# Two-layer hybrid encoder on one core: 512-column and 256-column matmuls of a weight piece sorted into runs

## The chip, the core and the metric

The kernel runs on 1 core of one Trainium2 chip. The metric is the device time of one execution in microseconds (us). Before the change the median of three runs is 747.52 us (747.17 to 747.56). Columns, partitions and shapes are written as the profile writes them: 128x512 is 128 partitions by 512 elements.

## What is computed

A hidden state of 256 tokens by 1024 features goes through two layers. The first has a mixer of two attention groups (windowed attention, and latent attention behind low-rank inputs), the second a mixer of three dilated attention windows. Each is followed by an MLP with a squared ReLU, and a last RMS norm ends it. All data are float32.

```python
def reference(x, ...):
    for layer in range(DEPTH):                       # DEPTH = 2
        xn = rms_norm(x, norm_mix[layer])
        if layer % 2 == 0:
            x = x + even_mixer(xn, ...)
        else:
            x = x + odd_mixer(xn, ...)
        x = x + sq_relu_mlp(rms_norm(x, norm_mlp[layer]), mlp_w1[layer], mlp_w2[layer])
    return rms_norm(x, norm_final)

def sq_relu_mlp(xn, w1, w2):                         # 1024 -> 4096 -> 1024
    return jnp.square(jax.nn.relu(xn @ w1)) @ w2

def odd_mixer(xn, w_in, w_o, cos_f, sin_f):          # queries, keys, values of 3 groups, 16 heads
    hcat = (xn @ w_in).reshape(b, s, DIL_GROUPS, 3, DIL_HEADS, HEAD_DIM)
    q = apply_rope(hcat[:, :, :, 0], cos_f, sin_f)
    k = apply_rope(hcat[:, :, :, 1], cos_f, sin_f)
    return dilated_attention(q, k, hcat[:, :, :, 2]) @ w_o
```

## The kernel before

**Split products.** Every float32 operand is split into a high part (rounded to the matmul type fp32r) and a low part (what is left), and a product is the sum of three: high by high, high by low and low by high. `split` makes the parts of a weight: a ScalarE copy (L201, "CAST whi<-raw") and then a VectorE subtraction (L202, "TENSOR_TENSOR wlo<-raw,whi"), in four parts of 512 columns for each weight piece of 128x2048. `weight()` hands out the next piece and lets the loads and splits run ahead of it; there are 4 buffers for raw pieces and 3 for each of whi and wlo. The loads are issued on SyncE's queue (SP).

**Two ways to issue the three products.** `mm3` (L205 to L207) issues three matmuls. Where the activations are the moving operand, two of the three can be one: `pair_tile` keeps the high and the low activations side by side, so that a single matmul of 512 columns gives whi by high in columns 0 to 255 of a PSUM bank and whi by low in columns 256 to 511, and a second matmul of 256 columns adds wlo by high to columns 0 to 255. This pair is used in two places:

- `up(j)` in `mlp` (L390 and L391), the MLP's first product: 16 weight pieces for each layer, and for each of them two banks (f = 0 and 1) with 8 pairs each (k = 0 to 7), 512 pairs in all. When a bank is done, ScalarE copies columns 256 to 511 out (L394, "side"), VectorE adds the two halves (L395, "u"), squares the positive part (L397) and splits it (L201 and L202, hh and hl).
- `gemm` in the `qk_steps` of `odd` (L905 and L906), the queries and keys of the second layer: 24 weight pieces, for each two banks with 8 pairs, 384 pairs in all. A bank's 8 pairs are cut into two steps of 4 (`half`), and other work is put between steps.

**Order.** Each engine executes its instructions in one fixed order. It comes from the order in which the code is written, changed by the scheduler of the framework, which moves instructions that could not start yet in its own model of time behind others that could. In the MLP it is `up(0)`, `up(1)`, `up(2)`, and then the second product of piece j (`down`, 24 matmuls of 512 columns through `mm3`) and `up(j + 3)` in turn. At the start of an MLP, `hand_over` adds the last products to the residual stream and prepares the activations in four blocks of two k (`join`: L301 on VectorE, then L241 on ScalarE for the high parts and L242 on VectorE for the low parts); `up(0)` therefore takes k in three ranges. In `odd`, `weave` puts the attention of one unit (scores L214 and L971, softmax, transposes L991, and `mix`, L1002 and L1007) between the steps that make the next unit's queries, keys and values.

**Other places that the change touches.** In `even`, `c_tail` normalises the low-rank inputs (L568, "cn") and returns a step that transposes them on TensorE (L576) and splits them (ch and cl). The list `main` holds the steps of this layer with a weight in time for each; the two transposing steps stand ahead of `main` and in its second place. `mix` in `odd` takes one PSUM bank for each half of the tokens. `finish` ends the kernel: the last 128 tokens are multiplied by the gain as they come (L504, "xg"), and when the reciprocal root of the norm is there (L232, on GpSimd), VectorE scales columns 0 to 511 (L506) for a store on SP's queue (L507), and ScalarE scales columns 512 to 1023 (L508) for a store on its own queue (L509).

Of the kernel before, what the change touches and what calls it, by code (L numbers as in the profile page):

```python
# [16 lines left out]
F32 = mybir.dt.float32  # L17
# [6 lines left out]
P = 128  # L24
# [44 lines left out]
def trunk(ctx, tc, a, out):  # L69
# [304 lines left out]
    def mlp(mp, xT, s, invert, tail, make_down, beside=lambda j: None):  # L374
# [4 lines left out]
        def up(j):  # L379
            w = weight()  # L380


            pu = [bank("w") for _ in range(2)]

            ranges = [range(4), range(4, 6), range(6, 8)] if j == 0 else [range(8)]
            for ks in ranges:
                for f in range(2):
                    for k in ks:
                        c = slice(k * 256 + f * P, k * 256 + f * P + P)
                        nc.tensor.matmul(two(pu[f]), w[0][:, c], xT[2][:, k], start=k == 0, stop=False)  # L390
                        nc.tensor.matmul(pu[f][:, 0:T], w[1][:, c], xT[0][:, k, :], start=False, stop=k == KT - 1)  # L391
# [48 lines left out]
    def finish(mp, xT, s):  # L440
# [49 lines left out]
        xg = [scratch([512], "xg") for _ in range(2)]  # L490
        residual(1, HALF[1], accs[3])
        for i, (c0, c1) in enumerate(((0, 512), (512, 768), (768, D))):
# [11 lines left out]
            nc.vector.tensor_tensor(xg[c0 // 512][:, c0 % 512:c0 % 512 + c1 - c0], v, g[:, c0:c1], op=ALU.mult)  # L504
        r = rsqrt(ss[:, 3:4], "x")
        nc.vector.tensor_scalar(xg[0], xg[0], r, None, ALU.mult)  # L506
        nc.sync.dma_start(out[P:T, HALF[0]], xg[0])  # L507
        nc.scalar.activation(xg[1], xg[1], AF.Copy, scale=r)  # L508
        nc.scalar.dma_start(out[P:T, HALF[1]], xg[1])  # L509


    def even(ep):
# [289 lines left out]
        turn_c[0]()  # L802
# [4 lines left out]
        main.insert(1, (0, turn_c[1]))  # L807
# [19 lines left out]
    def odd(op, xT, s):  # L827
# [64 lines left out]
        def qk_steps(d, js=QK_ORDER):  # L892
# [4 lines left out]
            def gemm(b, f, half):  # L897
# [5 lines left out]
                for k in range(4 * half, 4 * half + 4):  # L903
                    ws = slice((f * KT + k) * P, (f * KT + k + 1) * P)
                    nc.tensor.matmul(two(pq), wh[:, ws], xp[:, k], start=k == 0, stop=False)  # L905
                    nc.tensor.matmul(pq[:, 0:T], wl[:, ws], xh[:, k, :], start=False, stop=k == KT - 1)  # L906
# [51 lines left out]
        def attention(u, d):  # L958
# [36 lines left out]
            def mix(out_tag):  # L995
                pvo = [bank(out_tag) for _ in range(NT)]
                v0, v12 = values_of(u)
                for i in range(NT):
                    for kk in range(NT):
                        for j in range(2):  # L1000
                            cs = slice(64 * j, 64 * j + 64)
                            nc.tensor.matmul(pvo[i][cs, 0:P], v0[:, kk, cs], turned[i, j][:, kk, :], start=kk == 0, stop=False)  # L1002
                    for c in range(2):
                        qs = slice(64 * c, 64 * c + 64)
                        for j in range(2):
                            cs = slice(64 * j, 64 * j + 64)
                            nc.tensor.matmul(pvo[i][cs, qs], v12[:, 2 * i + c, cs], turned[i, j][:, 2, qs], start=False, stop=c == 1)  # L1007
                with tc.high_priority(NORM_PRIO):
                    for i in range(NT):
# [153 lines left out]
```

## Time and profile before

| what | value |
|---|---|
| median of three runs | 747.52 us |
| the profiled execution's own time | 746.66 us |
| its span, first to last instruction | 744.8 us |
| TensorE (PE) | 737.3 us busy, 99% of the span, 4539 matmuls |
| VectorE (DVE) | 539.9 us, 72% |
| ScalarE (ACT) | 473.6 us, 64% |
| GpSimd (POOL) | 8.3 us, 1% |
| granted TensorE clock, mean | 0.999 |
| HBM | 127.16 MB read, 172 GB/s over the span |

How to read what follows. A row of the timeline has the start of an instruction (or of several of one kind, merged, with their count), how long it took, and its line and operands. Matmuls are pipelined: one starts while the one before it is still in the array, so the busy time of a matmul (0.39 us for 512 columns) is longer than the distance to the next one's start. Since the profile models the ends of matmuls, all arithmetic on matmuls uses distances from start to start, called steps here. PEld is the engine row of the weight loads: every matmul has one of its own.

### The profile page before, as it was taken

Reading aid. Unit: us, or ns where it says so; the run is one execution under the profiler, and the core shown is the slowest. Engines: PE = TensorE matmul, PEld = TensorE weight load, DVE = VectorE, ACT = ScalarE, POOL = GpSimd, SP = SyncE. Lnnn points to the kernel's source line nnn. Section 1 sums busy time; section 2 is a strip of 40 time slices with the busy share of each in tenths; the row PEclk is TensorE's granted clock in tenths of the full one; section 3 lists DMA queues with packets and bytes.
Section 4 is the critical chain, followed back from the end, with each engine's and each line's share of the span. In section 5 each row is a group of like instructions: output and inputs, shape, how many; then the busy total and the mean of one; then the engine's idle time right before and its main releaser. Section 6 shows DMA issues by size and latency. Waiting matters only on the chain.

```text
span 744.8 us, 12006 instructions
## 1 busy us (share of the span) xinstructions
PE 737.3 (99%) x4539; PEld 634.8 (85%) x4539; DVE 539.9 (72%) x1109; ACT 473.6 (64%) x1027; POOL 8.3 (1%) x20
## 2 busy tenths in 40 slices
PE   9999999999999999999999999999999999999996
PEld 7998998888888887888888888888898888888885
DVE  6778858766666667689968886899558765665664
ACT  7788866554554556468877768687856544554541
POOL 0100000000000001000000000000000000000000
PEclk9999999999999999999999999999999999999999
DMA  9772334565555554645654555455545556555501
GB/s 292 309 272 97 118 113 166 175 222 178 187 201 178 191 196 152 234 159 172 213 209 144 191 175 180 136 194 169 194 148 181 194 191 205 184 177 191 193 13 56
DMA packets 24585, 133.17 MB, mean 179 GB/s; under 512 B 3664, under 2 KB 4688, under 8 KB 10192
## 3 DMA queue, kind: packets, MB, share of 16 engines
q1 hardware_dynamic: 24384, 132.15, 51.4%
q8 instruction: 35, 0.57, 0.3%
q10 hardware_dynamic: 144, 0.26, 0.1%
q14 instruction: 22, 0.18, 0.1%
HBM read 127.16 MB, written 1.05 MB: 172 GB/s over the span
## 4 chain that ended last, share of the span: by engine, by line
PE 97%; issue 1%; ACT 1%; DVE 0%; POOLq 0%; POOL 0%
PE w L390 16%; PE acc L205 13%; PE acc L207 13%; PE acc L206 13%; PE acc L905 12%; PE w L391 8%; PE acc L906 6%; PE acc L553 3%; PE w L214 1%; PE w L991 1%; PE w L205 1%; PE w L207 1%; PE w L763 1%; PE w L206 1%; PE w L971 1%
## 5 line engine op out<-in xcount | busy, mean ns | idle before, releaser
L202 DVE TENSOR_TENSOR wlo<-raw,whi 128x512 fp32r<-128x512 f32 (+2 forms) x471 | 304.6, 680 | 128.7 <-ACT whi L201 128.0
L201 ACT CAST whi<-raw 128x512 fp32r<-128x512 f32 (+2 forms) x471 | 262.4, 615 | 173.4 <-PE w L390 62.4
L390 PE MATMUL w<-pair,whi 128*128 128x512 f32 x512 | 182.2, 397 | 0.0
L391 PE MATMUL w<-pair,wlo 128*128 128x256 f32 x512 | 144.2, 282 | 0.0
L905 PE MATMUL acc<-pair,whi 128*128 128x512 f32 x384 | 139.2, 403 | 0.0
L390 PEld LDWEIGHTS w<-pair,whi 128*128 128x128 f32 x512 | 96.5, 189 | 23.1
L906 PE MATMUL acc<-pair,wlo 128*128 128x256 f32 x384 | 108.1, 282 | 0.0
L205 PE MATMUL acc<-whi,hh 128*128 128x512 f32 x250 | 98.2, 393 | 0.0
L207 PE MATMUL acc<-whi,hl 128*128 128x512 f32 x250 | 97.9, 391 | 0.0
L206 PE MATMUL acc<-wlo,hh 128*128 128x512 f32 x250 | 97.8, 391 | 0.0
L391 PEld LDWEIGHTS w<-pair,wlo 128*128 128x128 f32 x512 | 96.1, 188 | 0.9
L905 PEld LDWEIGHTS acc<-pair,whi 128*128 128x128 f32 x384 | 72.4, 189 | 16.8 <-issue 0.2
L906 PEld LDWEIGHTS acc<-pair,wlo 128*128 128x128 f32 x384 | 72.3, 188 | 0.0
L207 PEld LDWEIGHTS acc<-whi,hl 128*128 128x128 f32 x250 | 47.0, 188 | 9.9
L205 PEld LDWEIGHTS acc<-whi,hh 128*128 128x128 f32 x250 | 47.0, 188 | 9.8
L206 PEld LDWEIGHTS acc<-wlo,hh 128*128 128x128 f32 x250 | 47.0, 188 | 8.9
L394 ACT COPY side<-w 128x256 f32<-128x256 f32 x64 | 23.6, 369 | 22.1 <-PE w L391 22.1
L205 PE MATMUL acc<-whi,pair 128*128 128x512 f32 x80 | 32.4, 405 | 0.0
L207 PE MATMUL acc<-whi,pair 128*128 128x512 f32 x80 | 31.5, 394 | 0.0
L206 PE MATMUL acc<-wlo,pair 128*128 128x512 f32 x80 | 31.2, 390 | 0.0
L395 DVE TENSOR_TENSOR u<-w,side 128x256 f32<-128x256 f32 x64 | 26.9, 420 | 3.7 <-ACT side L394 3.0
L201 ACT CAST hh<-hsq 128x512 fp32r<-128x512 f32 x32 | 19.9, 622 | 10.1 <-DVE hsq L397 10.1
(221 smaller groups left out, 1102.9 us busy)
## 6 DMA issues: line engine op xcount, KB each, us to landing
raw<-in_w SPq DMA_DIRECT2D x64, 1024.0 KB, 4.9
raw<-in_w_oqk SPq DMA_DIRECT2D x24, 1024.0 KB, 5.2
raw<-in_w_ov SPq DMA_DIRECT2D x12, 1024.0 KB, 4.9
raw<-in_w_qk SPq DMA_DIRECT2D x4, 1024.0 KB, 8.9
raw<-in_w_oe SPq DMA_DIRECT2D x4, 1024.0 KB, 5.0
sw<-qk SPq DMA_DIRECT2D x64, 64.0 KB, 2.1
raw<-in_w_oo SPq DMA_DIRECT2D x4, 1024.0 KB, 5.0
bias<-in_rpb SPq DMA_DIRECT2D x8, 256.0 KB, 3.9
```

The lines of the kernel that those rows point to most:

```text
L201: a = nc.scalar.copy(hi, src).ins
L202: return a, (eng or nc.vector).tensor_tensor(lo, src, hi.bitcast(F32), op=ALU.subtract).ins
L205: nc.tensor.matmul(o, sh, mh, start=first, stop=False)
L206: nc.tensor.matmul(o, sh, ml, start=False, stop=False)
L207: nc.tensor.matmul(o, sl, mh, start=False, stop=last)
L390: nc.tensor.matmul(two(pu[f]), w[0][:, c], xT[2][:, k], start=k == 0, stop=False)
L391: nc.tensor.matmul(pu[f][:, 0:T], w[1][:, c], xT[0][:, k, :], start=False, stop=k == KT - 1)
L394: nc.scalar.copy(side[:, f], pu[f][:, T:2 * T])
L395: nc.vector.tensor_tensor(u[:, f], pu[f][:, 0:T], side[:, f], op=ALU.add)
L553: nc.tensor.matmul(o[:, 0:n], xs[i], (w[1], w[1], w[2])[i], start=(k, i) == (0, 0), stop=(k, i) == (KT - 1, 2))
L905: nc.tensor.matmul(two(pq), wh[:, ws], xp[:, k], start=k == 0, stop=False)
L906: nc.tensor.matmul(pq[:, 0:T], wl[:, ws], xh[:, k, :], start=False, stop=k == KT - 1)
```

## The change

In `up` all 512-column matmuls of a weight piece come first, 16 in a row for both banks, and then all 256-column matmuls, 16 in a row; in `up(0)` the ranges of k are kept for the 512-column ones. In `gemm` the first step of a bank has the 512-column matmuls of k = 0 to 5, and the second step those of k = 6 and 7 and then all eight 256-column ones. In `even` the two transposing steps of the low-rank inputs move into the list `main`, to its third and fifth place. In `mix` of `odd` both halves of the tokens go to one bank, and one split of 256 columns takes the place of two of 128. At the end, `xg` is one tile, ScalarE scales and stores columns 768 to 1023, and VectorE scales columns 0 to 767, which SP's queue stores.

```diff
@@ up, in mlp
             ranges = [range(4), range(4, 6), range(6, 8)] if j == 0 else [range(8)]
+            cut_of = lambda k, f: slice(k * 256 + f * P, k * 256 + f * P + P)
             for ks in ranges:
                 for f in range(2):
                     for k in ks:
-                        c = slice(k * 256 + f * P, k * 256 + f * P + P)
-                        nc.tensor.matmul(two(pu[f]), w[0][:, c], xT[2][:, k], start=k == 0, stop=False)
-                        nc.tensor.matmul(pu[f][:, 0:T], w[1][:, c], xT[0][:, k, :], start=False, stop=k == KT - 1)
+                        nc.tensor.matmul(two(pu[f]), w[0][:, cut_of(k, f)], xT[2][:, k], start=k == 0, stop=False)
+            for f in range(2):
+                for k in range(KT):
+                    nc.tensor.matmul(pu[f][:, 0:T], w[1][:, cut_of(k, f)], xT[0][:, k, :], start=False, stop=k == KT - 1)
@@ finish
-        xg = [scratch([512], "xg") for _ in range(2)]
+        xg = mp.tile([P, D], F32, name="xg")
...
-        nc.vector.tensor_scalar(xg[0], xg[0], r, None, ALU.mult)
-        nc.sync.dma_start(out[P:T, HALF[0]], xg[0])
-        nc.scalar.activation(xg[1], xg[1], AF.Copy, scale=r)
-        nc.scalar.dma_start(out[P:T, HALF[1]], xg[1])
+        c = slice(768, D)
+        nc.scalar.activation(xg[:, c], xg[:, c], AF.Copy, scale=r)
+        nc.scalar.dma_start(out[P:T, c], xg[:, c])
+        c = slice(0, 768)
+        nc.vector.tensor_scalar(xg[:, c], xg[:, c], r, None, ALU.mult)
+        nc.sync.dma_start(out[P:T, c], xg[:, c])
@@ even
-        turn_c[0]()
...
-        main.insert(1, (0, turn_c[1]))
+        main[3:3] = [(0, turn_c[1])]
+        main[2:2] = [(0, turn_c[0])]
@@ gemm, in qk_steps of odd
+                cut_of = lambda k: slice((f * KT + k) * P, (f * KT + k + 1) * P)
...
-                for k in range(4 * half, 4 * half + 4):
-                    ws = slice((f * KT + k) * P, (f * KT + k + 1) * P)
-                    nc.tensor.matmul(two(pq), wh[:, ws], xp[:, k], start=k == 0, stop=False)
-                    nc.tensor.matmul(pq[:, 0:T], wl[:, ws], xh[:, k, :], start=False, stop=k == KT - 1)
+                for k in (range(0, 6), range(6, KT))[half]:
+                    nc.tensor.matmul(two(pq), wh[:, cut_of(k)], xp[:, k], start=k == 0, stop=False)
+                if half == 1:
+                    for k in range(KT):
+                        nc.tensor.matmul(pq[:, 0:T], wl[:, cut_of(k)], xh[:, k, :], start=False, stop=k == KT - 1)
@@ mix, in odd
-                pvo = [bank(out_tag) for _ in range(NT)]
+                pvo = bank(out_tag)
...
-                    for i in range(NT):
-                        split(*(z[:, u % 4, tok(i)] for z in mixed[u // 4]), pvo[i][:, 0:P])
+                    split(*(z[:, u % 4, :] for z in mixed[u // 4]), pvo[:, 0:T])
```

The orders below list an engine's instructions as they are issued: line, operation, output<-inputs, shape, and x with a count where equal ones follow each other. In the first, numbered names tell buffers apart.

First place: TensorE at the start of the first MLP, before. w_1673 and w_1674 are the banks of `up(0)` for f = 0 and 1, whi_1580 and wlo_1581 its weights, pair_1576 the activations.

```order
L391 MATMUL w_1673<-pair_1576,wlo_1581 128x256
L390 MATMUL w_1673<-pair_1576,whi_1580 128x512
L391 MATMUL w_1673<-pair_1576,wlo_1581 128x256
L390 MATMUL w_1674<-pair_1576,whi_1580 128x512
L391 MATMUL w_1674<-pair_1576,wlo_1581 128x256
L390 MATMUL w_1674<-pair_1576,whi_1580 128x512
```

The same place with the change; L391 is now the 512-column line and L394 the 256-column one, and w_1731, w_1732 and whi_1663 belong to `up(1)`.

```order
L391 MATMUL w_1673<-pair_1576,whi_1580 128x512 x4
L391 MATMUL w_1674<-pair_1576,whi_1580 128x512 x4
L391 MATMUL w_1731<-pair_1576,whi_1663 128x512 x3
L391 MATMUL w_1673<-pair_1576,whi_1580 128x512 x2
L391 MATMUL w_1674<-pair_1576,whi_1580 128x512 x2
L391 MATMUL w_1673<-pair_1576,whi_1580 128x512 x2
L391 MATMUL w_1674<-pair_1576,whi_1580 128x512 x2
L394 MATMUL w_1673<-pair_1576,wlo_1581 128x256 x8
L394 MATMUL w_1674<-pair_1576,wlo_1581 128x256 x8
L391 MATMUL w_1731<-pair_1576,whi_1663 128x512 x5
L391 MATMUL w_1732<-pair_1576,whi_1663 128x512 x8
```

The alternation of widths is gone, and the scheduler has put three matmuls of `up(1)` ahead of k = 4 and 5 of `up(0)`. From here on the order of an `up` is 16 rows of 512 columns and 16 of 256; in the second MLP one matmul of `up(1)` stands in that place instead of three.

Second place: TensorE in `odd`, before, where the first unit's scores (L214) fall between two steps of a bank (acc_3709).

```order
L905 MATMUL acc_3709<-pair_3139,whi_3636 128x512
L906 MATMUL acc_3709<-pair_3139,wlo_3637 128x256
L905 MATMUL acc_3709<-pair_3139,whi_3636 128x512
L906 MATMUL acc_3709<-pair_3139,wlo_3637 128x256
L214 MATMUL w_3718<-q0h_3258 128x256
L214 MATMUL w_3719<-q0h_3258 128x256
```

With the change (L911 is the 512-column line, L914 the 256-column one):

```order
L911 MATMUL acc_3667<-pair_3139,whi_3573 128x512 x8
L914 MATMUL acc_3667<-pair_3139,wlo_3574 128x256 x8
L911 MATMUL acc_3709<-pair_3139,whi_3636 128x512 x6
L214 MATMUL w_3716<-q0h_3258 128x256
L214 MATMUL w_3717<-q0h_3258 128x256
```

A bank's work is now a run of eight 512-column matmuls and a run of eight 256-column ones, and what falls between two steps cuts the first run after six.

Third place: ScalarE in `even` around the splits of the transposed low-rank inputs (ch), before:

```order
L800 COPY both<-w 128x256
L201 CAST ch<-w 128x3x128
L201 CAST whi<-raw 128x512 x3
L201 CAST ch<-w 128x3x128
L201 CAST qk_h<-q_448 128x512
L201 CAST whi<-raw 128x512 x4
```

With the change:

```order
L805 COPY both<-w 128x256
L201 CAST whi<-raw 128x512 x4
L201 CAST ch<-w 128x3x128
L201 CAST qk_h<-q_448 128x512
L201 CAST whi<-raw 128x512 x2
L201 CAST ch<-w 128x3x128
```

Four parts of a weight now stand ahead of the first of the two splits. On TensorE the first set of transposes moves behind 24 more matmuls of 256 columns, and 12 stand between the two sets as before.

More of the change, by code (lines that the diff above doesn't have):

```diff
@@ L503, in finish @@
                                                scale=1.0 / D, scalar=ss[:, 2:3], accum_out=ss[:, 3:4])
-            nc.vector.tensor_tensor(xg[c0 // 512][:, c0 % 512:c0 % 512 + c1 - c0], v, g[:, c0:c1], op=ALU.mult)
+            nc.vector.tensor_tensor(xg[:, c0:c1], v, g[:, c0:c1], op=ALU.mult)
         r = rsqrt(ss[:, 3:4], "x")
-        nc.vector.tensor_scalar(xg[0], xg[0], r, None, ALU.mult)
-        nc.sync.dma_start(out[P:T, HALF[0]], xg[0])
-        nc.scalar.activation(xg[1], xg[1], AF.Copy, scale=r)
-        nc.scalar.dma_start(out[P:T, HALF[1]], xg[1])
+        c = slice(768, D)
[4 more added lines that the diff above has]
+        nc.sync.dma_start(out[P:T, c], xg[:, c])
     def even(ep):
@@ L1001, in mix @@
                             cs = slice(64 * j, 64 * j + 64)
-                            nc.tensor.matmul(pvo[i][cs, 0:P], v0[:, kk, cs], turned[i, j][:, kk, :], start=kk == 0, stop=False)
+                            nc.tensor.matmul(pvo[cs, tok(i)], v0[:, kk, cs], turned[i, j][:, kk, :], start=kk == 0, stop=False)
                     for c in range(2):
@@ L1006, in mix @@
                             cs = slice(64 * j, 64 * j + 64)
-                            nc.tensor.matmul(pvo[i][cs, qs], v12[:, 2 * i + c, cs], turned[i, j][:, 2, qs], start=False, stop=c == 1)
+                            nc.tensor.matmul(pvo[cs, i * P + 64 * c:i * P + 64 * c + 64], v12[:, 2 * i + c, cs], turned[i, j][:, 2, qs], start=False, stop=c == 1)
                 with tc.high_priority(NORM_PRIO):
-                    for i in range(NT):
-                        split(*(z[:, u % 4, tok(i)] for z in mixed[u // 4]), pvo[i][:, 0:P])
+                    split(*(z[:, u % 4, :] for z in mixed[u // 4]), pvo[:, 0:T])
             return scores, [lambda v=(i, j): turn(*v) for i in range(NT) for j in range(2)], mix
```

## The prediction

> **What bounds the kernel now.** I read the page first (busy shares, clock, chain), then the waits of TensorE, then its timeline.
>
> ```profile
> PE 737.3 (99%) x4539; PEld 634.8 (85%) x4539; DVE 539.9 (72%) x1109; ACT 473.6 (64%) x1027; POOL 8.3 (1%) x20
> PEclk9999999999999999999999999999999999999999
> PE 97%; issue 1%; ACT 1%; DVE 0%; POOLq 0%; POOL 0%
> PE acc L117 <- DVE warm L112: 1.2, 1, 1.2
> ACT whi L201 <- PE w L390: 62.4, 28, 2.4
> DVE wlo L202 <- ACT whi L201: 128.0, 75, 3.7
> ```
>
> TensorE is 97% of the chain that ends last, at its full granted clock in every slice. The fourth line is the only wait that the view of TensorE's waits lists: nothing but the first memset ever holds it up. ScalarE's splits wait for TensorE to give buffers back (62.4 us), and VectorE's for ScalarE's. So the time is the sum of the steps of TensorE's matmuls, from start to start, and the change is worth what it does to these.
>
> ```profile
> L390 PE MATMUL w<-pair,whi 128*128 128x512 f32 x512 | 182.2, 397 | 0.0
> L905 PE MATMUL acc<-pair,whi 128*128 128x512 f32 x384 | 139.2, 403 | 0.0
> 181.08 0.39 PE L390 MATMUL w<-pair,whi 128*128 128x512 f32 x1
> 181.32 0.28 PE L391 MATMUL w<-pair,wlo 128*128 128x256 f32 x1
> 181.44 0.39 PE L390 MATMUL w<-pair,whi 128*128 128x512 f32 x1
> ...
> 186.73 0.39 PE L205 MATMUL acc<-whi,hh 128*128 128x512 f32 x1
> ...
> 345.21 0.40 PE L905 MATMUL acc<-pair,whi 128*128 128x512 f32 x1
> ...
> 348.04 0.40 PE L905 MATMUL acc<-pair,whi 128*128 128x512 f32 x1
> ```
>
> The groups give the counts: 512 pairs in the MLPs and 384 in the second layer. From 181.08 to 186.73 one `up` issues 16 pairs in 5.65 us, and from 345.21 to 348.04 the second layer issues 8 in 2.83: about 353.5 ns a pair in both. The first rows split a pair: some 0.235 us for the 512 columns and 0.12 for the 256.
>
> **Runs, as far as the trace has them.** First the 24 matmuls of 512 columns behind that `up`, then 36 of 256 columns that follow a 512-column one in the first layer.
>
> ```profile
> 188.35 0.39 PE L206 MATMUL acc<-wlo,hh 128*128 128x512 f32 x1
> ...
> 191.98 0.39 PE L207 MATMUL acc<-whi,hl 128*128 128x512 f32 x1
> ...
> 25.84 0.40 PE L553 MATMUL acc<-wlo,pair 128*128 128x512 f32 x1
> 26.07 0.28 PE L205 MATMUL w<-pair,whi 128*128 128x256 f32 x1
> ...
> 26.88 0.28 PE L206 MATMUL w<-pair,whi 128*128 128x256 f32 x1
> ...
> 27.79 0.28 PE L205 MATMUL w<-pair,whi 128*128 128x256 f32 x1
> ...
> 30.05 0.28 PE L207 MATMUL w<-pair,wlo 128*128 128x256 f32 x1
> ```
>
> A run begins uneven and settles. The first 7 steps of the 512-column run (186.73 to 188.35) take 231 ns each, the next 16 (to 191.98) 227. In the 256-column run 7 steps (26.07 to 26.88) take 116 ns each, the first 15 (to 27.79) 114.7, the last 20 (to 30.05) 113. Sorted by width, a settled pair would be 227 + 113 = 340 ns where it is 353.5 now. The trace also has slower runs:
>
> ```profile
> 299.94 0.39 PE L205 MATMUL w<-whi,pair 128*128 128x512 f32 x1
> ...
> 305.44 0.40 PE L205 MATMUL acc<-whi,pair 128*128 128x512 f32 x1
> 108.00 0.28 PE L207 MATMUL acc<-obh,wlo 128*128 128x256 f32 x1
> ...
> 113.30 0.28 PE L207 MATMUL acc<-obh,wlo 128*128 128x256 f32 x1
> ```
>
> 24 steps of 512 columns in 5.50 us are 229 ns each and never settle; 45 steps of 256 in 5.30 us are 118. Which of these the new runs take isn't shown, since weights as the stationary operand with 512 columns of activations moving occur only in alternation. For the 256 columns I take the run at 26.07, which has the same operands (weights stationary, activations moving) and the same entry, and for the 512 columns of an `up` the settled 227, since an `up` follows 24 matmuls of `down` in that state.
>
> **Term 1, the MLPs.** An `up` becomes 15 steps of 227 (3.405), one step from 512 to 256 columns (0.235), 15 of 114.7 (1.72) and one back (0.12): 5.48 us where 5.65 stand, 0.17 less. Times 32: **-5.4 us**. Bounds: settled throughout (227 and 113) -6.2; the starts' 231 and the slow 118 give 5.59 and -1.9.
>
> **Term 2, the second layer.** A bank has only 8 and 8, so its runs are all start: 7 x 231 + 235 + 7 x 116 + 120 = 2.784 us where 2.83 stand, 0.046 less. Times 48 banks: **-2.2 us**. Bounds: settled -4.6, with 118 in the 256-column run -1.5. The transposes and scores that fall between steps cut a run as they cut the alternation; I add nothing for them.
>
> **Term 3, the start of each MLP.** Sorted, `up(0)` needs k = 4 to 7 sooner. The rows are VectorE's low parts for k = 4 to 7, in each MLP, and the first matmul of `up(0)`.
>
> ```profile
> 113.42 0.40 PE L390 MATMUL w<-pair,whi 128*128 128x512 f32 x1
> 115.09 1.68 DVE L242 SCALAR_TENSOR_TENSOR pair<-gx,pair 128x256 fp32r<-128x256 f32 x4
> 557.95 0.39 PE L390 MATMUL w<-pair,whi 128*128 128x512 f32 x1
> 559.64 1.67 DVE L242 SCALAR_TENSOR_TENSOR pair<-gx,pair 128x256 fp32r<-128x256 f32 x4
> ```
>
> Four low parts in 1.68 us are 0.42 each. In the first MLP k = 4 is ready at 115.5 and would be wanted after 8 steps, at 115.25; the three matmuls of `up(1)` that the new order puts there move that to 115.9, behind it. In the second one matmul stands there: k = 4 is wanted at 560.0 and ready at 560.06, k = 7 wanted about 561.25 and ready at 561.3. With what a signal takes I put **+0.2 us** for both. Bounds: 0, and +0.6 if the second shifts by a whole low part and the filler doesn't help.
>
> **Term 4, the low-rank inputs.** TensorE's timeline where the second set of transposes stands:
>
> ```profile
> 33.48 0.28 PE L206 MATMUL acc<-pair,whi 128*128 128x256 f32 x1
> 33.59 0.28 PE L207 MATMUL acc<-pair,wlo 128*128 128x256 f32 x1
> 33.87 0.52 PE L576 MATMUL w<-ident,cn 128*128 128x128 f32 x3
> ```
>
> The step from 33.59 is 0.28 us against 0.11 before it. Later by 24 matmuls (2.7 us) "cn" is long there: **-0.15 us** (0 if the step is only the turn to another operand type). What is turned is next used many steps later, so its delay is hidden.
>
> **Term 5, the end.** The last scaling and the stores behind it:
>
> ```profile
> 737.23 0.42 ACT L475 ACTIVATE junk<-xt 128x256 f32<-128x256 f32 x1 [1.22 <-DVE xt L472]
> 740.60 0.49 DVE L506 TENSOR_SCALAR xg<-xg,rstd 128x512 f32<-128x512 f32 x1 [0.45 <-POOL rstd L232]
> 740.60 0.72 ACT L508 ACTIVATE xg<-xg,rstd 128x512 f32<-128x512 f32 x1 [2.86 <-POOL rstd L232]
> out<-xg SPq DMA_DIRECT2D x1, 256.0 KB, 2.1
> out<-xg ACTq DMA_DIRECT2D x1, 256.0 KB, 2.5
> L201 ACT CAST whi<-raw 128x512 fp32r<-128x512 f32 (+2 forms) x471 | 262.4, 615 | 173.4 <-PE w L390 62.4
> ```
>
> ScalarE's half sets the end. With 256 columns it takes about 0.5 (0.42 for another of that shape), VectorE with 768 about 0.62 (its 0.49 and half of it at most more), so the later store is issued 0.1 us sooner; but both together still move 512 KB, and one is now 384. I take **-0.05 us**, between -0.2 and +0.25 (that half as long again). The single split in `mix` shortens ScalarE and VectorE, which wait for TensorE: nothing. In the new order ScalarE has six whi parts ahead of an `up`'s first "side"; that delays hh and hl, which `down` uses only three pieces later: nothing either, and without that cover 0.6 us for a part (the last row).
>
> **Sum.** -5.4 - 2.2 + 0.2 - 0.15 - 0.05 = -7.6 us. Made against the profiled execution (746.66 us, 744.8 of them the span) it gives 739.1; the median of the runs is 0.86 above that execution, and with the same distance the median is **739.9 us**. All bounds on the good side give -6.2 - 4.6 - 0.15 - 0.2 = -11.15 (736.4), on the bad side -1.9 - 1.5 + 0.6 + 0.25 = -2.55 (745.0).
>
> **A rule that speaks against it.** The Trainium skill, "TensorE: Matmul & The Clock Gate", section "Back-to-back issue gap", gives the gap by the width alone (518 cycles for 512 columns, 262 for 256, at 2.4 GHz). By it a pair costs the same in any order, 325 ns, and terms 1 and 2 are nil, which is the first rival below. The trace disagrees so far: steps of 512 columns are 227 ns before their like and 235 before 256 columns.
>
> **Rivals.** *Width alone* (0.09): the 235 and 118 ns belong to these operands (weights stationary, 512 columns of activations moving), not to the alternation. For it: all rows of that operand pair alternate. Against it: 256-column matmuls with the same operands take 113 in a run. Terms 1 and 2 vanish: 747.5 us. *Unsettled runs* (0.15): the runs stay at 229 and 118, as at 299.94 and 108.00. An `up` is then 5.56 us, -2.9 in all, and with -1.5 for the second layer the time is 743.1. *The weight load shows* (0.06, the slower side):
>
> ```profile
> L391 PEld LDWEIGHTS w<-pair,wlo 128*128 128x128 f32 x512 | 96.1, 188 | 0.9
> ```
>
> A weight load takes 188 ns in its row. In the alternation every second one lies under a 512-column matmul, in the new runs 15 of 16 lie under 256 columns. If a 256-column step grew to that load, a pair would be 227 + 188, 61 ns over the 353.5, and the 816 inner pairs (32 x 15 and 48 x 7) cost 50 us: 797 us. It decides from 126.5 ns a step. Against it: the 256-column runs above, each matmul with its own load, at 113 to 118. That same section says that the spacing is set by both the load and the matmul.
>
> **How the numbers follow.** The forecast has 0.70. Faster by over 0.2% (1.5 us, about what a measurement of this kernel can tell from no change) takes it and the unsettled runs: 0.85; same 0.09; slower 0.06. The range is 736.4 to 745.0 us: it holds the first two cases and leaves out the other 0.15 and little more.
>
> **What would show it.** In the profile after: an `up` of 5.48 us from its first 512-column start to that of `down`; steps of 227 and 113 to 115 inside the runs; a bank of the second layer at 2.78 us; no new wait in the view of TensorE's waits, and no step of over 0.4 us at the starts of the MLPs; the transposes of "cn" right behind their forerunner. Wrong would be 235 ns between two 512-column starts, or a step of 0.12 and more throughout the 256-column runs.

## The result and the profile after

The changed kernel takes 742.42 us (median of six runs, 741.60 to 743.44) where the kernel before takes 747.38 in runs beside it (six, 747.17 to 747.56): a ratio of 0.9936, with a 95% interval of 0.9926 to 0.9946, or 5.0 us less. The forecast was 7.6 us less. The profiled execution has its own time of 742.68 us and a span of 740.9, about 4 less than the span before.

From the page after: the busy line of each engine, the granted clock, the chain's shares by engine.

```profile
PE 732.5 (99%) x4539; PEld 628.5 (85%) x4539; DVE 538.6 (73%) x1100; ACT 471.4 (64%) x1020; POOL 8.4 (1%) x20
PEclk9999999999999999999999999999999999999999
PE 94%; DMA 1%; DVE 1%; issue 1%; ACT 1%; SPq 1%; POOLq 0%; POOL 0%
```

TensorE's three rows and one of VectorE's in the view of waits (waited for what: us in all, times, longest).

```profile
PE acc L117 <- DVE warm L112: 1.2, 1, 1.2
PE w L979 <- DVE q L940: 0.7, 1, 0.7
PE acc L205 <- DVE obl L202: 0.2, 1, 0.2
DVE wlo L202 <- ACT whi L201: 67.6, 44, 3.7
```

TensorE is still what the time is made of, at the same clock, with as many matmuls. It now has two small waits that it did not have. VectorE's wait for ScalarE's high parts fell from 128.0 to 67.6 us; that pays nothing, since TensorE's rows list no wait for a weight's parts, before or after.

TensorE's timeline gives one `up` (rows of one line merged: start, us, count at the end), and then a bank and the start of the next in the second layer.

```profile
180.54 3.89 PE L391 MATMUL w<-pair,whi 128*128 128x512 f32 x16
184.27 1.99 PE L394 MATMUL w<-pair,wlo 128*128 128x256 f32 x16
186.10 0.39 PE L205 MATMUL acc<-whi,hh 128*128 128x512 f32 x1
...
326.91 2.02 PE L911 MATMUL acc<-pair,whi 128*128 128x512 f32 x8
328.77 1.07 PE L914 MATMUL acc<-pair,wlo 128*128 128x256 f32 x8
329.69 2.02 PE L911 MATMUL acc<-pair,whi 128*128 128x512 f32 x8
```

The `up` takes 5.56 us from its first start to that of `down` (5.65 before, 5.48 forecast): 16 steps of 512 columns in 3.73 us, 233 ns each, and 16 of 256 columns in 1.83, 114 each. The bank takes 2.78 us, as forecast (2.83 before). So the 256-column run came out as forecast, and the 512-column run of the `up` did not.

Mean steps of all starts in the trace, in ns, where nothing else stands between the two matmuls:

| step | before | after | forecast after |
|---|---|---|---|
| 512 columns, MLP | 234.6 (x512, to 256) | 234.2 (x480, to 512) | 227 |
| 256 columns, MLP | 118.8 (x484, to 512) | 114.6 (x480, to 256) | 114.7 |
| 512 columns, second layer | 240.6 (x384) | 240.3 (x324) | 231 inside a run |
| 256 columns, second layer | 118.6 (x356) | 114.8 (x336) | 116 |
| `down`, 512 columns | 229.1 (x717) | 228.6 (x717) | not counted |

(The second layer's means hold some longer steps where other work has just cut a run.) Sorting saved 4 ns on each 256-column matmul and nearly nothing on the 512-column ones. The 114.6 is the mean of two kinds of runs: 27 of the MLPs' 32 runs of 256 columns step by 114 ns, five by 118. What remained to explain was why a 512-column run of `up` steps by 233 where `down` steps by 227.

### The profile page after: what moved, and what is told of

Same layout as the page of the kernel before. It is cut to its first block, busy times and chain, and to the rows that moved or that the text cites. A ratio compares the mean times of both kernels' runs of the same rounds, so it can differ in the third digit from the quotient of the medians.

```text
span 740.9 us, 11984 instructions
## 1 busy us (share of the span) xinstructions
PE 732.5 (99%) x4539; PEld 628.5 (85%) x4539; DVE 538.6 (73%) x1100; ACT 471.4 (64%) x1020; POOL 8.4 (1%) x20
## 4 chain that ended last, share of the span: by engine, by line
PE 94%; DMA 1%; DVE 1%; issue 1%; ACT 1%; SPq 1%; POOLq 0%; POOL 0%
PE w L391 16%; PE acc L205 13%; PE acc L207 13%; PE acc L206 13%; PE acc L911 11%; PE w L394 8%; PE acc L914 5%; PE acc L558 2%; PE w L214 1%; PE w L999 1%; PE w L205 1%; PE w L768 1%; PE w L207 1%; PE w L206 1%; PE w L979 1%
## 5 line engine op out<-in xcount | busy, mean ns | idle before, releaser
L202 DVE TENSOR_TENSOR wlo<-raw,whi 128x512 fp32r<-128x512 f32 (+2 forms) x471 | 303.0, 679 | 68.2 <-ACT whi L201 67.6
L391 PE MATMUL w<-pair,whi 128*128 128x512 f32 x512 | 125.0, 395 | 0.0
L391 PEld LDWEIGHTS w<-pair,whi 128*128 128x128 f32 x512 | 95.2, 187 | 22.9 <-DVE pair L242 0.6
L911 PE MATMUL acc<-pair,whi 128*128 128x512 f32 x384 | 101.6, 401 | 0.0
L911 PEld LDWEIGHTS acc<-pair,whi 128*128 128x128 f32 x384 | 67.7, 188 | 12.4 <-issue 0.2
L394 PEld LDWEIGHTS w<-pair,wlo 128*128 128x128 f32 x512 | 63.4, 188 | 2.9
L394 PE MATMUL w<-pair,wlo 128*128 128x256 f32 x512 | 63.9, 277 | 0.0
L914 PEld LDWEIGHTS acc<-pair,wlo 128*128 128x128 f32 x384 | 51.2, 188 | 4.4
L914 PE MATMUL acc<-pair,wlo 128*128 128x256 f32 x384 | 51.9, 278 | 0.0
L990 ACT ACTIVATE pp<-sn,dmn 128x384 f32<-128x384 f32 x32 | 19.7, 614 | 9.8 <-DVE dmn L988 8.9
```

Source lines behind the costliest of these rows:

```text
L202: return a, (eng or nc.vector).tensor_tensor(lo, src, hi.bitcast(F32), op=ALU.subtract).ins
L391: nc.tensor.matmul(two(pu[f]), w[0][:, cut_of(k, f)], xT[2][:, k], start=k == 0, stop=False)
L394: nc.tensor.matmul(pu[f][:, 0:T], w[1][:, cut_of(k, f)], xT[0][:, k, :], start=False, stop=k == KT - 1)
L911: nc.tensor.matmul(two(pq), wh[:, cut_of(k)], xp[:, k], start=k == 0, stop=False)
L914: nc.tensor.matmul(pq[:, 0:T], wl[:, cut_of(k)], xh[:, k, :], start=False, stop=k == KT - 1)
L990: nc.scalar.activation(pp, sn, AF.Exp, bias=mn, scale=-1.0, accum_out=z)
```

## The experiments

**The parts alone.** Each of these four kernels is the kernel before with some parts of the change, taken from it as they stand. *p_mlp* has the sorted `up` alone:

```diff
             for ks in ranges:
                 for f in range(2):
                     for k in ks:
-                        nc.tensor.matmul(two(pu[f]), w[0][:, c], xT[2][:, k], ...)
-                        nc.tensor.matmul(pu[f][:, 0:T], w[1][:, c], xT[0][:, k, :], ...)
+                        nc.tensor.matmul(two(pu[f]), w[0][:, cut_of(k, f)], xT[2][:, k], ...)
+            for f in range(2):
+                for k in range(KT):
+                    nc.tensor.matmul(pu[f][:, 0:T], w[1][:, cut_of(k, f)], xT[0][:, k, :], ...)
```

> The kernel before with one part of the change alone: the MLP's `up` sorted by width (512-column run, then 256-column run, per half). Prediction's term T1 as it was sized (512-column steps of 227 ns, an `up` of 5.48 us): -5.4 us, so about 742.0 us. Theory W (what the changed kernel's profile shows: 512-column steps of 233 ns in `up`, an `up` of about 5.54 us): 32 x -0.11 = -3.5 us, about 743.9 us. Rival (the gain of the change is not in `up` at all, but in the transposes and the tail): within 0.5 us of before. The profile should again show mean steps of 233 to 235 ns between two 512-column matmuls of `up`.

Measured: 743.99 us against 746.94, ratio 0.9959 (0.9946 to 0.9973): -2.95 us, with a mean 512-column step of 234.2 ns. The prediction's size of term 1 (-5.4) falls.

*p_odd* has the sorted second layer alone:

```diff
-                for k in range(4 * half, 4 * half + 4):
-                    nc.tensor.matmul(two(pq), wh[:, ws], xp[:, k], ...)
-                    nc.tensor.matmul(pq[:, 0:T], wl[:, ws], xh[:, k, :], ...)
+                for k in (range(0, 6), range(6, KT))[half]:
+                    nc.tensor.matmul(two(pq), wh[:, cut_of(k)], xp[:, k], ...)
+                if half == 1:
+                    for k in range(KT):
+                        nc.tensor.matmul(pq[:, 0:T], wl[:, cut_of(k)], xh[:, k, :], ...)
```

> The kernel before with another part alone: the second layer's query/key products sorted by width, all else as before. Prediction's term T2: -2.2 us, about 745.2 us. Theory W (steps of 233 ns, a bank of 2.77 us, but one new wait of some 0.8 us on VectorE in the scores of that stage): -1.2 to -1.5 us, about 746.0 us. Rival (the wait belongs to the moved transposes or the one-bank mix, not to the sorted products): -2.2 us or more and no TensorE wait over 0.5 us at the scores' line in this run.

Measured: 745.38 us, ratio 0.9977 (0.9969 to 0.9986): -1.56 us, and no TensorE wait is listed at the scores. The interval, -2.3 to -1.0 us, holds both the -2.2 of term 2 and the -1.2 to -1.5 of theory W, so the time doesn't tell them apart.

*p_rest* has everything else (the two transposing steps later in `main`, `mix` in one bank, the tail in 256 and 768 columns):

```diff
-        turn_c[0]()
...
-        main.insert(1, (0, turn_c[1]))
+        main[3:3] = [(0, turn_c[1])]
+        main[2:2] = [(0, turn_c[0])]
```

> The kernel before with all the rest of the change and neither sorted product: transposes of the low-rank inputs later, mix in one bank, tail cut 256/768. Prediction's terms T4 and T5 and the mix: -0.2 us, about 747.2 us. Theory W (the stages of the changed kernel's profile: first part +0.2, even part -0.1, tail +0.1): +0.2 us, about 747.6 us. Rival (these parts carry the new wait at the scores of the second layer, or part of the gain): 1 us or more off before, either way.

Measured: 747.08 us, ratio 1.0001 (0.9993 to 1.0010): no difference that can be measured.

*p_both* has both sorted products and no other part.

> The kernel before with both sorted products and nothing else of the change (transposes of the low-rank inputs, mix and tail as before). Theory sum (both sorted parts carry the whole gain, and the rest of the change adds nothing): -3.0 and -1.6 us, about 742.4 us, as the changed kernel itself, in the MLPs' stages -1.4 us each and in the second layer's query/key stage -1.2 to -1.8 us. Theory wait (the TensorE wait of some 0.7 us at the scores, in the changed kernel and not in the one with the second layer's products alone, comes of the rest of the change): no TensorE wait over 0.3 us at the scores here, and that stage at -1.7 us. Rival (the wait comes when both sorted parts are there, by the order in which loads and splits fall): the wait is here too and the stage at -1.2 us.

Measured: 742.34 us against 746.85, ratio 0.9938 (0.9924 to 0.9952): -4.5 us, the sum of the two parts, and as fast as the whole change. The query/key stage of the second layer is 1.75 us shorter than before (first start of that stage to the first of the output product), against 1.17 in the changed kernel. TensorE's timeline at the scores, first in the changed kernel:

```profile
477.86 0.28 PE L214 MATMUL w<-q0h,q0l 64*128 64x256 f32 x2
478.81 1.09 PE L979 MATMUL w<-k,q 128*64 128x128 f32 x16 [0.66 <-DVE q L940]
```

and in *p_both*:

```profile
478.16 0.28 PE L214 MATMUL w<-q0h,q0l 64*128 64x256 f32 x2
478.54 1.09 PE L975 MATMUL w<-k,q 128*64 128x128 f32 x16
```

The wait is in the changed kernel and not with the sorted products alone. The chain of the changed kernel (start, us) shows what it hangs on: a transfer of 4.05 us for the rotary swap, then VectorE's row up to "q".

```profile
468.04 4.05 DMA sw<-qk
...
478.15 0.61 DVE q L940
```

The wait goes with the length of that transfer, which differs between executions of the same instructions. *m_steps*, *m_align* and *m_table* below run the changed kernel's instructions up to its last store. In their executions the same transfer took 3.77, 2.02 and 3.10 us, and the step at these scores 0.66, 0.38 and 0.38 us, where it is 0.94 above; *p_both* had 2.05 us and 0.38. So the theory that the rest of the change brings the wait is not borne out, although its number came true in *p_both*. Before the change the step was 0.21 us, with a transfer of 4.23, so the kernel had more room there. Whether the sorted products alone would wait behind so slow a transfer is not shown, since none fell on them.

**Which operand makes 233.** *m_steps* is the changed kernel with rows of 24 extra 512-column matmuls behind its last store. One row as it stands:

```diff
+            for i in range(24):
+                nc.tensor.matmul(two(o[0]), cut(wa[0], i % 16, P), px[:, i % 8], start=i == 0, stop=i == N - 1)
```

> The changed kernel with nine rows of 24 extra 512-column matmuls behind its last store, results unused; the time itself grows by about 9 x 24 x 0.23 = 50 us and is not read. Per row the step between two starts is read, the first few left out. In order: (1) weights stationary, token pair moving, one bank, as in the sorted `up`; (2) the same, two banks in turn; (3) weights stationary and weights moving; (4) weights stationary, hidden moving; (5) one weight slice stationary throughout, pair moving; (6) hidden stationary, pair moving; (7) hidden stationary, weights moving, as in the down products; (8) pair stationary, weights moving; (9) two weight tiles' slices stationary, weights moving. Theory operand (the moving pair makes 233 in place of 227 ns): rows 1, 2, 5, 6 at 233, rows 3, 4, 7, 8, 9 at 227. Theory stationary (the weight slices as the stationary operand make it): rows 1 to 4 and 9 at 233, rows 6 to 8 at 227. Theory bank (a long run into one bank makes it): row 2 at 227, all others at 233. Theory history (what ran before sets it): all rows alike.

The timeline of its rows (names: moving operand first, then stationary). From one start to the next row's are 24 steps.

```profile
734.86 5.77 PE L522 MATMUL w<-pair,whi 128*128 128x512 f32 x24
740.47 5.76 PE L524 MATMUL w<-pair,whi 128*128 128x512 f32 x24
746.07 5.62 PE L526 MATMUL w<-whi 128*128 128x512 f32 x24
751.53 0.39 PE L528 MATMUL w<-hh,whi 128*128 128x512 f32 x1
...
756.97 5.76 PE L530 MATMUL w<-pair,whi 128*128 128x512 f32 x24
762.57 5.76 PE L532 MATMUL w<-pair,hh 128*128 128x512 f32 x24
768.17 5.62 PE L534 MATMUL w<-whi,hh 128*128 128x512 f32 x24
773.63 5.66 PE L536 MATMUL w<-whi,pair 128*128 128x512 f32 x24
779.12 2.88 PE L538 MATMUL w<-whi 128*128 128x512 f32 x12
```

The rows with the pair moving (L522, L524, L530, L532) take 5.60 or 5.61 us, 233 ns a step, with one bank or two, with walking or fixed weights, with weights or hidden stationary. The rows with weights or hidden moving (L526, L528, L534) take 5.44 to 5.46, settled at 227. Theories bank, stationary and history fall; the moving pair makes it. But the last row is the expectation's miss: with the pair stationary (L536) the step is 229, neither.

**Is it the pair's place?** The pair starts 64 bytes past a multiple of 128 in its partition; weights and hidden (hh and hl) start at multiples of 128. These places are those that the program allots to its tiles; the trace does not show them. *m_align* puts rows behind the last store again, with operands moved by a few bytes; *a_align* and *b_align* put an unused tile ahead of the activations (the pair at a multiple of 128) and one behind them (the weights, by 128 in all, too).

```diff
+    act.tile([P, 16], F32, name="gap_a")
     gx = act.tile([P, 4 * KT + KT * T], F32, name="gx")
...
+    gap.tile([P, 16], F32, name="gap_b")
     wraw = ctx.enter_context(tc.tile_pool(name="wraw", bufs=RAWBUFS))
```

> The changed kernel with fifteen rows of 24 extra matmuls behind its last store, results unused, weight slices stationary; per row the settled step is read. Moving: (1) pair as it lies (64 bytes past a multiple of 128), (2) pair 64 bytes on, (3) pair 32 bytes on, (4) pair 128 bytes on; (5) weights as they lie (a multiple of 128), (6) weights 64 bytes on, (7) weights 32 bytes on; (8) weights with the stationary slices 64 bytes on, (9) the same 32 bytes on; (10) weights, 256 columns, (11) the same 64 bytes on; (12) weights, 512 and 256 columns in turn, (13) the same 64 bytes on; (14), (15) 128 columns, as they lie and 64 bytes on. Theory address: 233 ns in rows 1, 4, 6 and 227 ns in rows 2, 5; rows 3 and 7 tell the grain (32 bytes); rows 12 and 13 tell whether 353.5 ns for two widths in turn is of the place (340 and 353.5) or of the change of width (353.5 in both). Theory tile: rows 1 to 4 at 233, rows 5 to 9 at 227.

Measured, settled steps in ns by the number of the row: 233 (1), 227 (2), 233 (3), 229 (4), 227 (5), 229 (6), 233 (7), 233 (8), 233 (9); with 256 columns 120 (10) and 118 (11); the two widths in turn 347 (12) and 349 (13) for both together; with 128 columns 112 (14, 15). The place decides, not the tile: the pair 64 bytes on is as cheap as the weights, and the weights 64 or 32 bytes off are as dear as the pair. But the rule was wrong: the pair 128 bytes on took 229, and moving only the stationary slices (8, 9) made weights dear too.

> The changed kernel with two unused tiles of 64 bytes per partition: one ahead of the activations, so that the token pair starts at a multiple of 128 bytes in place of 64 past one (as the weights and the hidden pieces do already), one behind them, so that the weights keep their place. Same instructions in the same order. Theory address (a moving operand that starts 64 bytes past a multiple of 128 costs 7 ns more per 512 columns): 512-column steps of 227 ns in `up` and in the second layer's query/key products, so 480 x 6.6 + 336 x 5.5 = 5.0 us less than the changed kernel, about 737.2 us, with an `up` of 5.45 to 5.48 us. Theory tile (something else in the pair makes 233, its data, its many readers): steps stay 233, time within 0.5 us of the changed kernel's 742.4 us. Rival (the walk of the weight slices beside it): also no change.

Measured: 747.84 us against 746.86, ratio 1.0012 (1.0003 to 1.0021). The whole gain of the change is gone by two unused tiles. `up`'s 512-column steps stay at 233.5, and its 256-column ones went from 114.6 to 118.7. Those of the second layer rose from 114.8 to 118.7 and those of the output products from 120.7 to 123.4; the three are 4.2 us together. Theory address falls.

> The kernel before with the same two unused tiles, nothing else. Theory address, with the dear step of the old order caused by the pair's place alone: a 512- and a 256-column matmul together take 227 + 113 = 340 in place of 353.5 ns, so 512 + 384 pairs x 13 ns = 11 us less, about 736 us, and sorting would then be worth nothing. Theory address with a separate cost of changing width: the pair keeps most of its 353.5 ns, and the time falls by 0 to 4 us, about 743 to 747 us. Theory tile: no change, 747 us.

Measured: 747.52 us, ratio 1.0006 (0.9997 to 1.0015): the same tiles cost the kernel before nothing measurable. That number is no proof of theory tile, since steps did move and cancelled: in the MLPs 512 columns went from 234.6 to 231.0 ns and 256 columns from 118.8 to 119.6, while the output products' 256-column steps rose from 120.7 to 123.5.

**A rule in the distance.** All these rows of 512 columns, and the 512-column steps of `up`, `down` and the products that make the second layer's values, in the changed kernel and in *a_align*, fit one reading: take the start of the moving operand minus that of the stationary one, in bytes of a partition, modulo 256. In the changed kernel the pair is at 64 and weights and hidden are at 128: `up` has -64 (233 ns), `down` 0 (227), the values +64 (229). *a_align* gave `up` a distance of 128. *m_table* tries the distances with weights as both operands, so that nothing but the place differs.

```diff
+        st = lambda i, at: wa[:, 128 * (i % 12) + at:128 * (i % 12) + at + P]
+        mv = lambda i, at, n: wb[:, 512 * (i % 3) + at:512 * (i % 3) + at + n]
+            for i in range(24):
+                nc.tensor.matmul(o[:, 0:512], st(i, 0), mv(i, 16, 512), start=i == 0, stop=i == 23)
```

> The changed kernel with extra rows of matmuls behind its last store, weight slices both stationary and moving, results unused. First nine rows of 24 matmuls with 512 columns, moving operand 0, 32, 64 ... 256 bytes further than the stationary one (modulo 512); nine with 256 columns, the same; then 512 columns with both 64 bytes on, and with stationary 128 and moving 64 on; 256 columns with stationary 64 on; rows of 16 with 512 and 16 with 256 columns, as an `up` has them, with distances (-64, -64), (0, 0), (0, -64), (0, -192), (0, -128), each twice; last four rows of 512 and 256 columns in turn, at distances -64, 0, -192, -128. Theory difference: for 512 columns 227 at distance 0, 229 at 64, 233 at 32 and 128 to 224 (192 is -64, 224 is -32); 256 tells whether it is modulo 256 (227) or 512 (233); both 64 on as distance 0: 227; stationary 128 and moving 64 on as -64: 233. For 256 columns 120 at 0 and 118 at 64 and no more than 115 at -64 behind a 512-column row. Theory address (each operand's own place): both 64 on gives 233, not 227. In turn: 353.5 for the two at -64, as in the kernel before.

Rows of its timeline: 512 columns at distances 32, 64, 96, then 224 and 256; 256 columns at 0, 32, 64, then at 192 (which is -64), 224 and 256; 512 columns with both operands 64 bytes on, then stationary 128 and moving 64 on; 256 columns with the stationary operand 64 bytes on.

```profile
739.85 5.77 PE L523 MATMUL w<-whi 128*128 128x512 f32 x24
745.45 5.67 PE L525 MATMUL w<-whi 128*128 128x512 f32 x24
750.96 5.77 PE L527 MATMUL w<-whi 128*128 128x512 f32 x24
...
773.39 5.76 PE L535 MATMUL w<-whi 128*128 128x512 f32 x24
778.99 5.63 PE L537 MATMUL w<-whi 128*128 128x512 f32 x24
784.45 3.04 PE L539 MATMUL w<-whi 128*128 128x256 f32 x24
787.32 3.00 PE L541 MATMUL w<-whi 128*128 128x256 f32 x24
790.15 2.99 PE L543 MATMUL w<-whi 128*128 128x256 f32 x24
...
801.52 2.89 PE L551 MATMUL w<-whi 128*128 128x256 f32 x24
804.25 3.00 PE L553 MATMUL w<-whi 128*128 128x256 f32 x24
807.08 3.03 PE L555 MATMUL w<-whi 128*128 128x256 f32 x24
809.95 5.65 PE L557 MATMUL w<-whi 128*128 128x512 f32 x24
815.44 5.76 PE L559 MATMUL w<-whi 128*128 128x512 f32 x24
821.03 2.99 PE L561 MATMUL w<-whi 128*128 128x256 f32 x24
```

Settled over the last twelve steps of a row: 512 columns take 226.7 at distance 0, 233.3 at 32, 228.9 at 64, 233 to 234 at 96 to 224, and 226.7 again at 256. Both operands 64 on is 226.7 (L557), 128 against 64 is 233.3 (L559): the distance counts, not the place of either. For 256 columns the order is another: 120.0 at 0, 96 and 256, 117.5 to 119 at most other distances, and the least, 113.3, at 192, that is -64 (L551: 2.73 us to the next row, 114 ns a step), which is the distance of `up`. But here the distance alone does not decide. The row with the stationary operand 64 bytes on (L561) is at -64 too, and it took 117.8, where the expectation had at most 115. Rows as an `up` has them were as divided: at -64 the 256-column run settled at 117.8 the first time and at 113.3 the second, and behind a 512-column run at distance 0 it took 117.8 both times. The two widths in turn took 353.5 ns at distances -64, 0 and 64, and 351 at 128; *m_align* had 347 and 349 for two of them, so that number isn't fixed by the distance.

**The rule in the kernel.** *c_same* is the changed kernel with 64 bytes of tiles allotted ahead of the pair, not behind it, so that pair and weights are at distance 0.

```diff
-        ms = work.tile([P, NT], F32, tag="ms", name="ms")
+        ms = const.tile([P, NT], F32, tag="ms", name="ms", bufs=2)
```

> The changed kernel with one tile of 64 bytes (two buffers of `ms`) allotted ahead of the activations in place of behind them: the pair moves up by 64 bytes, weights and hidden stay. Same instructions in the same order. Theory difference: the 512-column step hangs on the byte distance between the moving and the stationary operand's start, modulo 256 at least; in all rows so far 0 gave 227, +64 gave 229, every other (-64, 32, -32, 128) 233 ns, and with the pair here at distance 0 from the weights the 512-column steps of `up` become 227: 480 x 6.6 = -3.2 us. The 256-column steps go from 114.6 to the 120 that distance 0 showed in the extra rows: 480 x 5.4 = +2.6 us in the MLPs, and in the second layer's short rows -1 and +1.8 us; in all 742.4 +- 1 us, with both steps changed in the profile. Theory address (each operand's own place, 128 bytes apart, decides): no reading of the aligned kernel fits it, which had 233 with both at multiples of 128; it says 233 here too and no change. Rival (256-column steps stay at 114.6 since they follow other work than in the extra rows): 738.2 us.

```profile
181.91 3.79 PE L391 MATMUL w<-pair,whi 128*128 128x512 f32 x16
185.54 2.08 PE L394 MATMUL w<-pair,wlo 128*128 128x256 f32 x16
187.45 0.40 PE L205 MATMUL acc<-whi,hh 128*128 128x512 f32 x1
```

Measured: 16 steps of 512 columns in 3.63 us (227 each, 233 in the changed kernel) and 16 of 256 in 1.91 (119.5, 114.4 there); over all of them the means are 227.9 and 119.5. Both moved as the distance says, with the same instructions in the same order: -3.0 us and +2.3 us in the MLPs. So the place of the pair, against the weights, makes the 233. The time was outside the expected margin, 744.39 us against 747.08 beside it, ratio 0.9959 (0.9945 to 0.9973), some 2 us more than the changed kernel: I had counted the 256-column products of the MLPs and of the second layer's queries and keys, and left out those of the rest (the first layer's, and the output products, whose mean went from 120.7 to 124.3), which paid 3.6 to 5 ns a step.

*y_place* tries to have both: 0 for the 512-column products and -64 for the 256-column ones, by unused tiles before and behind the pair and between the high and the low weights. (The quarters in its expectation are the tiles oah, oal, obh and obl, which the output products read.) *b_place* is the kernel before with the same tiles.

```diff
+    act.tile([P, 16], F32, name="gap_a")
     gx = act.tile([P, 4 * KT + KT * T], F32, name="gx")
...
+    gap_c.tile([P, 16], F32, name="gap_c")
+    wsl = ctx.enter_context(tc.tile_pool(name="wsl", bufs=WBUFS))
```

> The changed kernel with four unused tiles (64, 192, 64, 192 bytes) that set the operands' starts, modulo 256 bytes, to: pair 128, high weights 128, low weights 192, hidden 128, the quarters 64 as before. Same instructions in the same order. Theory difference: 512-column matmuls of `up` and of the second layer at distance 0 (227 ns a step: -3.0 us and -1.0 us against the changed kernel), their 256-column ones at -64 (115 ns, unchanged), a third of the down products at +64 (229 in place of 227: up to +0.6 us), the 256-column products of pair by high weights at 0 (+0.6 us) and of quarter by low weights at -128 (+0.8 us): together -2.0 us, about 740.4 us, with mean steps of 228 ns between two 512-column matmuls of `up` and 115 ns between two 256-column ones. Theory address (no rule in the distance): no change from 742.4 us, or worse. Rival (the cheap step needs all operands of neighbouring matmuls at distance 0): 256-column steps at 118 to 120 again and 744.5 us.

```profile
181.69 3.83 PE L397 MATMUL w<-pair,whi 128*128 128x512 f32 x16
185.35 2.05 PE L400 MATMUL w<-pair,wlo 128*128 128x256 f32 x16
187.24 0.40 PE L211 MATMUL acc<-whi,hh 128*128 128x512 f32 x1
```

Measured: 746.42 us, ratio 0.9994 (0.9985 to 1.0003): no gain over before is left. The 512-column steps fell (16 in 3.66 us, mean 229.5; uneven at some 231 for eight steps, then 227), but the 256-column ones took 117.7 at the distance that gives 114.6 in the changed kernel, and `down`, of whose three products one had moved to +64, went from 228.6 to 233.1 over all three, which is 3.2 us. The 256-column steps are as the rival had them, the time is not (744.5). So the rule holds for 512-column runs at one distance once they have settled; in a row with mixed distances a step also hangs on its neighbours, and I have no rule for it. The expectation overlooked the rows of *m_table* that had shown the 117.8.

> The kernel before, with 512 and 256 columns in turn in `up` and in the second layer's query/key products, and the same four unused tiles as the other kernel of this pair. Theory difference with a cost of changing the width that no distance takes away (the extra rows had 353.5 ns for the two in turn at distances -64, 0 and 64 alike): within 1.5 us of the kernel before, about 747 to 748.5 us. Rival (distance 0 for 512 and -64 for 256 columns makes the turn cheap, 227 + 115 = 342 ns): 896 pairs x 11 ns = 10 us less, about 737 us, and sorting would not have been needed.

Measured: 747.00 us, ratio 0.9998 (0.9989 to 1.0007). The number is as expected, the reason is not: the two widths in turn fell to 230.5 + 117.1 = 348 ns, and `down`, at 233.0, took back what that gave in the MLPs (2.8 of 2.9 us).

No version here beats the changed kernel; *p_both* equals it with less of the change.

## Why the prediction was right, and where it was not

**What bounds the kernel**: right. The time followed TensorE's steps, and every experiment's time can be read from them.

**Term 1, the MLPs**, was -5.4 us and measured -2.95 alone. The step that failed: "for the 512 columns of an `up` the settled 227, since an `up` follows 24 matmuls of `down` in that state". The state is not carried over. `down` has its operands at distance 0 and `up` at -64, and `up` went to 233 at once; that even lies outside the bound taken for it (231). At 234.2 for 227 the 480 inner steps cost 3.5 us of the forecast. The 256-column run came out as sized (114.6 for 114.7), in part by luck: the forecast took the uneven start of one run, and the kernel has 27 runs at 114 and five at 118. Two things not counted gave a little back: the step out of the run took 114 and not 120 (0.2 us), and `down` begins more evenly behind it (229.1 to 228.6, 0.4 us). That makes -2.5, inside the interval of *p_mlp* (-4.0 to -2.0). The text had named 235 ns between two 512-column starts as the sign of being wrong; 234.2 is next to it. The gain that was left is that of the 256-column steps. They came out 3.4 ns under the 118 of the bad bound, 1.6 us in all, and without that the term would have left its own bounds; that the time lies in the range is luck as far as the 512 columns go.

**Term 2, the second layer**, was -2.2 and measured -1.56 alone. An unbroken bank came out at 2.78 us as forecast, in both parts (1.86 us for eight steps of 512 columns, 0.92 for eight of 256). Over all 48 banks the steps that begin with these matmuls add up to 138.34 us before and 136.38 in *p_odd*, 1.96 less, so the term was sized some 0.2 too high. That is 0.042 us for each of the 36 banks in one piece and 0.037 for each of the 12 that other work cuts, for which "I add nothing" was near enough. Most of the saving is in the 256 columns: the 512-column mean hardly moved (240.6 to 240.3), and 336 steps of 256 columns at 3.8 ns less are 1.3 us. What lowers the 1.96 is in part the step at one unit's scores, 0.17 us longer in *p_odd* and, with the slow transfer, 0.73 in the changed kernel's profiled execution; "no new wait" was wrong by that much. The interval of *p_odd* does not exclude the -2.2.

**Term 3, the MLP starts**, was +0.2: right. At the second MLP 17 matmuls of L391 stand between these two starts, 4.21 us where 17 x 233 ns are 3.96, so 0.25 us; in the first no step shows a delay.

```profile
555.22 4.38 PE L391 MATMUL w<-pair,whi 128*128 128x512 f32 x17
559.43 1.98 PE L394 MATMUL w<-pair,wlo 128*128 128x256 f32 x16
```

**Terms 4 and 5** were -0.15 and -0.05, too small to measure apart (*p_rest*: 1.0001). The step onto the second set of low-rank transposes is 0.12 us where it was 0.28, as term 4 had it. They stand without a wait now, where *p_mlp* and *p_both*, which have them at the old place, list a wait of 0.3 us for "cn". The tail was mis-signed within its bounds: from TensorE's last matmul to the end it is about 0.1 us longer; the larger store landed in 2.7 us where both halves took 2.1 and 2.5.

**The rivals.** *Width alone* was half right: the 234.6 ns of the 512-column step do belong to that operand pair, or rather to where it lies, and the order changes next to nothing in them; the 118.8 of the 256-column step belonged to the alternation. Its source, the table in the Trainium skill's "TensorE: Matmul & The Clock Gate", section "Back-to-back issue gap", which gives the gap by width alone, does not hold here: the same 512-column matmul took 227, 229 or 233 ns by the distance of its operands. *Unsettled runs* had named 5.56 us for an `up`, which is what it takes, from other parts (233 and 114, not 229 and 118), and its 743.1 us is nearer than the forecast. *The weight load shows* is out: 256-column steps of 114 with a load each.

## What to carry to other kernels

When a step is borrowed from another run of the same shape, check that its operands are the same tiles in the same places: here the two runs differed by 6 ns in 227, which was nearly half of the forecast gain (3.5 of 7.6 us). Time the parts of a change apart, since here two of five parts carried all that could be measured. A pad or a tile allotted elsewhere can move this kernel by 5 us with not one instruction changed, so compare versions whose buffers lie at the same places, or treat the layout as part of the change.

## What the runs showed of the hardware

The step between equal fp32r matmuls of 512 columns hangs on the distance between the starts of the moving and the stationary operand in a partition, modulo 256 bytes as far as it was tried (0 to 256 bytes in steps of 32): a settled run takes 227 ns at 0, 229 at 64, and 233 to 234 at the other multiples of 32. With 256 columns it is 120 at 0, 118 at 64, and 113 or 118 at -64, so the two widths are cheapest at different distances. What chooses between the 113 and the 118, which the same operands can have, is not shown. Why the distance counts is not shown either, and neither is a rule for rows of mixed distances, where one product of three at another distance brought `down` from 228.6 to 233.1 ns.
